# Stores on the GpSimd queue, bias tables loaded whole from reversed rows, two-head matmuls and a reordered first norm in a fused two-layer kernel

## The chip, the cores and the metric

One core of a Trainium2 chip runs the whole program. The metric is device time in microseconds (us) of one execution, the median over several.

## The reference

Two layers act on `x` of 1024 tokens by 1024 channels, in fp32, one after the other.

Layer 1: `h = rmsnorm(x) * norm_gain`, `proj = h @ w_in`, and two mixers. Eight heads of 64 attend over all tokens with two key heads (norm and axial rotation on q and k). Eight heads attend over a neighbourhood of 8 rows by 16 columns of a 64-wide grid, with a relative bias. Both are gated by `silu`, joined, multiplied by `w_out` and added to `x`; a final rmsnorm follows.

Layer 2: `rms_norm`, `h @ w_in_2`, and again two mixers: a gated delta rule (four heads of 128, chunks of 64, a triangular solve per chunk, a state carried along the tokens) and dilated attention:

```python
DILATED_PATTERNS = ((128, 1), (512, 4), (2048, 16))      # window, dilation
step = qi - kj + blk                                     # per residue class, current and previous block
scores = q . k + rel_bias[:, t5_bucket(step * r)]        # masked to 0 <= step <= window / r
lse = logsumexp(scores); p = exp(scores - lse); o = p @ v
o = sum over patterns of softmax(lse over patterns) * o  # then * silu(gate)
```

Both are joined, multiplied by `w_out_2` and added.

## The kernel before

**Numbers.** Projections split both operands into a high and a low part (`whi`, `wlo` for weights, `hh`, `hl` for activations) and sum three matmuls. Token tiles are 128 rows; activations are transposed on TensorE so that channels lie on partitions, and the evacuation writes `hh` on ScalarE and `hl = t - hh` on VectorE.

**Stages**, by the time of the profile: 0 to 49 us load of `x`, norm and 64 transposes (the loop at L547 to L575); up to 550 us the projections of layer 1 (`fill1`) woven with the first attention; up to 760 us neighbourhood attention woven with the output product; up to 850 us the rest of that product and the second norm; up to 1380 us the delta rule (`delta_main`), woven with the projections of layer 2 (`fill2`); then dilated attention (`jobs_c`, head pairs j = 0 to 3) woven with the last output product, to the end.

**What sets the order.** The program is written as two streams, `main` and `fill`, which `share` weaves by the TensorE time each has spent; a scheduler then fixes one static order for each engine. An engine, and each DMA queue, takes its instructions strictly in that order: a DMA issue that waits holds all issues behind it. Three names choose the queue: `ld` (loads) and `st` (stores) both issue from SyncE (SP), `gl` from GpSimd (POOL); `gl` carries only the loads of q, k and v for neighbourhood attention (L795, L796, L824). Stores and the loads that read them back go through tensors in device memory (`qa_d`, `bq_d`, `raw_d`, `ab_d`, `tb_d`, `n_d`, `yp_d`, `o_d`; names ending in `_d`).

**First norm.** `norm_gain` is loaded broadcast to 128 partitions (`ng`, L559). For tiles 2 to 7 VectorE multiplies each by it (L563); for tiles 0 and 1 the multiplication is fused with that by the row's scale (L574); the other scalings are three on VectorE (L572) and three on ScalarE (L570).

**Dilated attention.** `tables_c(j)` makes the bias tables of a pair of heads. `r_d` holds one row of 1024 numbers per head; table k needs, on partition p, the row shifted by p and reversed. A load brings the shifted piece into `trc` with step 1 (L1487), and a ScalarE copy writes it reversed into `tab` (L1489): six of each per pair, 24 in all. `item` (L1556) is one block of 128 queries of two heads: scores `s` (a high and a low pass per head), then on VectorE `Pc = -(s + tab)` with its row minimum (L1568), exponential on ScalarE (L1570), transposes, `PTc` copied on ScalarE (L1581), and `po = PTc^T vc` (P·V, 64 columns per head), copied to `N` or `Nst` (L1592). With dilation 8 (`nkt == 1`: 8 items) and the first blocks an item has one key block of 128, otherwise two. Results of two patterns go through `n_d` and are merged per half of the tokens in `union_c` (L1631 on).

**Memory.** The pool `wk` is closed after the delta rule (named "pd") and opened as "pc" over the same bytes; a new tile waits until the old tiles under it are free.

Of the kernel before, what the change touches and what calls it, by code (L numbers as in the profile page):

```python
# [32 lines left out]
NT = 8  # L33
KC = 8
# [28 lines left out]
XPR = 5000  # L63
XS = 1
LASTC = {1: 6, 2: 7}
# [11 lines left out]
CP = 'S'  # L77
CO = 'V'
CHP = 0
# [18 lines left out]
def shape_constants():  # L98
# [45 lines left out]
    for x in range(256):  # L144
# [3 lines left out]
        else:  # L148
            oh[32, 768 + x] = NEG
    return {"c1": c1, "c2": c2, "oh": oh}  # L150


@with_exitstack
def hybrid_kernel(ctx: ExitStack, tc: tile.TileContext, A, out, dbg=None, upto=99):
# [30 lines left out]
    ld = nc.sync.dma_start  # L185
    gl = nc.gpsimd.dma_start
    st = nc.sync.dma_start
    dbg = dbg or {}
# [352 lines left out]

    r_d = dp.tile([8, 1024], F32, name="r_d")


    w1 = A["w_in"][0]
    H = {}
    hr.open("h1")  # L547
    H1 = Tr(hr, KC)
    with tc.tile_pool(name="xp", bufs=2, reuse_waits="tile") as xp:
        ng = xp.tile([128, 1024], F32, name="ng", bufs=1)  # L550
        for b in range(0, NT, 2):
            ss = sm.tile([128, 2], F32, name="ssx")
            xg = []
            for i in (b, b + 1):
                xt = xp.tile([128, 1024], F32, name="xt", bufs=8)
                with tc.high_priority(XPR):
                    ld(xt, grid(x_in, i))
                    if i == 0:
                        ld(ng, dram(A["norm_gain"], 0, [[0, 128], [1, 1024]]))  # L559
                scr = xp.tile([128, 1024], F32, name="sqrow", bufs=1)  # L560
                S.activation(scr, xt, AF.Square, accum_out=ss[:, i - b:i - b + 1])
                if b:
                    V.tensor_tensor(xt, xt, ng, op=OP.mult)  # L563
                xg.append(xt)
            rs = rs_of(ss, 2, 1.0 / 1024)
            for i in (b, b + 1):
                xn = xg[i - b]
                r1 = rs[:, i - b:i - b + 1]
                if b and i % 2 and XS:
                    S.activation(xn, xn, AF.Copy, scale=r1)  # L570
                elif b:
                    V.tensor_scalar(xn, xn, r1, None, op0=OP.mult)  # L572
                else:
                    V.scalar_tensor_tensor(xn, xn, r1, ng, op0=OP.mult, op1=OP.mult)  # L574
                H1.put(xn, i)  # L575

    def make_bias():
        rb = wk.tile([33, 8], F32, name="rb")
        V.memset(rb, 1.0)
        tb8 = wk.tile([8, 32], F32, name="tb8")  # L580
        ld(tb8, A["rel_bias_2"])
        tb = tbank()
        PE.transpose(tb[0:32, 0:8], tb8, ident[0:8, 0:8])
        V.tensor_copy(rb[0:32], tb[0:32, 0:8])
        oh = wk.tile([33, 1024], F32, name="oh")
        ld(oh, A["oh"])
        rr = wk.tile([8, 1024], F32, name="rr")
# [4 lines left out]
        ld(r_d, rr)  # L592


    wk.open("rpp")
    if 1:
# [192 lines left out]
    def prep_b(j, B):  # L789
# [4 lines left out]
        for a in range(2):  # L794
            gl(k2[64 * a:64 * a + 64], dram(bq_d[j], (2 + a) * 128 * 1024, [[1024, 64], [64 * 1024, 2], [1, 1024]]))  # L795
        gl(vv, bv_d[j].rearrange("(t p) c -> p t c", p=128))  # L796
        if j == 0:
# [18 lines left out]
    def attn_b(j, B, live, then=None):  # L816
# [243 lines left out]
    def fill1():  # L1060
        ws, _ = load_w(w1, [(512, 0, 1, 256), (0, 0, 1, 256)])
# [91 lines left out]
    def delta_main():  # L1153
# [20 lines left out]
        def main2():  # L1174
# [164 lines left out]
            def chain(u):  # L1339
# [5 lines left out]
                for k in range(2):  # L1345
# [3 lines left out]
                    V.tensor_reduce(ac, am.rearrange("p t (b c) -> p t c b", c=16), op=OP.add, axis=AX.X)  # L1349
                    ld(dram(ab_d[u], k * 8192, [[16, 128], [2048, 4], [1, 16]]), ac)  # L1350
                Ab = wk.tile([64, 16, 16], F32, name="Ab")
# [6 lines left out]
                for r in range(1, 16):  # L1358
# [4 lines left out]
                    yield Y1  # L1363
                ld(tb_d[u], Tn.rearrange("p r c -> p (r c)"))

# [103 lines left out]
    yp_d = dp.tile([1024, 1024], F32, name="yp_d")  # L1469
    X, alt = {}, [0]  # L1470

# [72 lines left out]
    def jobs_c(j):  # L1544
# [5 lines left out]
        def values(n, *ap):  # L1550

            v = wk.tile([128, 8, 2, 64], F32, name="vc", bufs=VCB)
            ld(v.rearrange("p t h d -> p (t h d)").rearrange("p (a b) -> p a b", a=n), dram(cv_d[j], 0, list(ap)))
            return [v[:, t] for t in range(8)]

        def item(q, k, vs, T, N, then=None):  # L1556
# [9 lines left out]
            P = wk.tile([128, 2, 256], F32, name="Pc", bufs=CB)  # L1566
            for h in range(2):
# [9 lines left out]
            PT = wk.tile([128, 4, 128], F32, name="PTc", bufs=CB)  # L1577
            t3 = by4(tb[:, 0:2 * nkt * 128])
# [10 lines left out]
            if CO[alt[0] % len(CO)] == "S":  # L1589
                S.activation(N[:, 0:128], o[:, 0:128], AF.Copy)  # L1590
            else:
                V.tensor_copy(N[:, 0:128], o[:, 0:128])  # L1592
            if then:
# [3 lines left out]
        def nst():  # L1597
            return wk.tile([128, 2, 132], F32, name="Nst", bufs=NSB)

# [31 lines left out]
    def union_c(j):  # L1631
        def union(N0, b):

            Ns = [N0[:, 4 * b:4 * b + 4]]
            for p in range(2):
                N = wk.tile([128, 4, 132], F32, name="N%d" % (p + 1))
                ld(N, n_d[j][p][512 * b:512 * b + 512].rearrange("(t p) c -> p t c", p=128))
# [33 lines left out]
    def main():  # L1671
# [51 lines left out]
```

## Time and profile before

| | |
|---|---|
| median of 3 runs (lowest, highest) | 1762.08 us (1745.34, 1762.79) |
| profiled execution, its span | 1749.34 us, 1747.6 us |
| mean granted TensorE clock | 0.937 of full (2.4 GHz) |
| busy: TensorE, VectorE, ScalarE, GpSimd | 1560.6 (89%), 1121.8 (64%), 785.3 (45%), 28.5 us (2%) |
| DMA | 204.79 MB, 38.4% of 16 engines by hardware queue, 4.9% by the software queue of GpSimd |

A row of the timeline gives start, duration, engine, line, operation, tiles and shape; in brackets the idle time before it and what ended it. `SPq` is an issue on SyncE's queue. `--windows` rows give for a stretch the busy time of each engine with instruction counts, the granted TensorE clock (1.00 is 2.4 GHz, 0.50 is 1.2 GHz) and the busy share of the 16 DMA engines. PE is TensorE, DVE is VectorE, ACT is ScalarE.

### The profile page before, as it was taken

How to read it: one execution, taken by the hardware profiler on the slowest of the kernel's cores; microseconds unless marked ns; L12 is line 12 of the kernel's file. 1: busy time of each engine (PE TensorE's matmuls, PEld its weight loads, DVE VectorE, ACT ScalarE, POOL GpSimd, SP SyncE). 2: the span in 40 equal slices, each digit the busy share in tenths (PEclk: the TensorE clock that was granted, in tenths of full speed). 3: DMA queues.
4: the chain of work that ended last, by engine and by line, in shares of the span. 5: the costliest groups of instructions: out<-in, count | busy, mean ns of one | idle time of the engine just before them, and what ended most of it. 6: DMA issues, size and time to landing. Idle time of an engine off the chain costs nothing. (4 is left out here: it accounts for less than half of the span.)

```text
span 1747.6 us, 27569 instructions
## 1 busy us (share of the span) xinstructions
PE 1560.6 (89%) x9362; PEld 1377.5 (79%) x9362; DVE 1121.8 (64%) x3469; ACT 785.3 (45%) x2189; POOL 28.5 (2%) x48
## 2 busy tenths in 40 slices
PE   1988999999999789996799999998999489899997
PEld 1877788989898677885677788887889478788985
DVE  5679866666573554558545768676677575767646
ACT  5235445445452432544344443534524352765631
POOL 0000000000001101100000000000000000000000
PEclk8999999999999889997899999999999879876999
DMA  7011121422226998875344323314322555433476
GB/s 173 17 61 51 56 80 63 102 79 56 83 71 162 199 256 194 223 208 145 76 113 98 96 74 85 97 51 108 91 61 71 166 174 162 136 93 87 119 229 219
DMA packets 212825, 204.79 MB, mean 117 GB/s; under 512 B 27363, under 2 KB 164763, under 8 KB 212684
## 3 DMA queue, kind: packets, MB, share of 16 engines
q1 hardware_dynamic: 202252, 188.34, 38.4%
q0 software_dynamic: 10432, 14.68, 4.9%
q8 instruction: 74, 1.21, 0.3%
q14 instruction: 67, 0.55, 0.1%
HBM read 131.83 MB, written 71.13 MB: 116 GB/s over the span
## 5 line engine op out<-in xcount | busy, mean ns | idle before, releaser
L172 PE MATMUL pw<-whi,hh 128*128 128x512 f32 (+2 forms) x1032 | 359.1, 350 | 10.5 <-DVE e L524 5.4
L172 PE MATMUL pw<-wlo,hh 128*128 128x512 f32 (+2 forms) x1032 | 357.1, 346 | 0.3 <-DVE wlo L355 0.3
L172 PE MATMUL pw<-whi,hl 128*128 128x512 f32 (+2 forms) x1032 | 356.3, 345 | 0.0
L172 PEld LDWEIGHTS pw<-whi,hh 128*128 128x128 f32 x1032 | 196.9, 192 | 31.9 <-DVE e L524 6.0
L172 PEld LDWEIGHTS pw<-wlo,hh 128*128 128x128 f32 x1032 | 197.8, 192 | 19.6 <-DVE wlo L355 0.5
L172 PEld LDWEIGHTS pw<-whi,hl 128*128 128x128 f32 x1032 | 197.4, 191 | 19.9
L355 DVE TENSOR_TENSOR wlo<-e,whi 128x512 fp32r<-128x512 f32 (+3 forms) x168 | 103.6, 624 | 73.3 <-ACT whi L354 72.3
L354 ACT ACTIVATE whi<-e 128x512 fp32r<-128x512 f32 (+3 forms) x168 | 95.3, 581 | 96.9 <-DMA e<-in_w_in_dram 71.0
L172 PE MATMUL pw<-hh,whi 128*128 128x512 f32 x320 | 129.8, 405 | 7.6 <-ACT whi L354 7.5
L172 PE MATMUL pw<-hl,whi 128*128 128x512 f32 x320 | 127.2, 398 | 0.0
L172 PE MATMUL pw<-hh,wlo 128*128 128x512 f32 x320 | 123.3, 399 | 0.0
L172 PEld LDWEIGHTS po<-vc,PTc 128*128 128x128 f32 x560 | 87.9, 228 | 12.1 <-DVE N L1592 5.4
L172 PE MATMUL po<-vc,PTc 128*128 128x64 f32 x560 | 90.2, 304 | 7.3 <-DVE N L1592 4.2
L172 PE MATMUL s<-k,qT 128*128 128x512 f32 (+1 forms) x282 | 90.1, 407 | 2.7 <-ACT PT L845 1.3
L1568 DVE CUSTOM_DVE_ANT_0 Pc<-s,tab 128x128 f32<-128x128 f32 (+1 forms) x192 | 59.6, 348 | 39.5 <-PE s L172 26.4
L172 PE MATMUL po<-PT,vv 128*128 128x256 f32 x512 | 75.9, 288 | 3.9 <-DVE PT L745 3.2
L172 PEld LDWEIGHTS pw<-hh,whi 128*128 128x128 f32 x320 | 61.1, 191 | 23.2 <-ACT whi L354 11.2
L172 PEld LDWEIGHTS po<-PT,vv 128*128 128x128 f32 x512 | 68.7, 193 | 8.7 <-DVE PT L745 5.1
L745 DVE TENSOR_TENSOR PT<-s,PT 128x512 fp32r<-128x512 f32 x77 | 52.3, 685 | 32.2 <-ACT PT L744 23.1
L736 ACT ACTIVATE P<-s,nm 128x512 f32<-128x512 f32 x77 | 52.6, 686 | 44.7 <-DVE nm L733 41.9
L840 ACT ACTIVATE Pb<-Pb,m 128x384 f32<-128x384 f32 x64 | 39.1, 612 | 73.3 <-DVE m L838 70.6
L172 PEld LDWEIGHTS pw<-hl,whi 128*128 128x128 f32 x320 | 61.2, 191 | 11.4
(398 smaller groups left out, 3364.8 us busy)
## 6 DMA issues: line engine op xcount, KB each, us to landing
e<-in_w_in_dram SPq DMA_DIRECT2D x72, 256.0 KB, 3.7
bq_d<-e SPq DMA_DIRECT2D x32, 256.0 KB, 2.2
qT<-bq_d POOLq DMA_DIRECT2D x32, 256.0 KB, 7.4
e<-in_w_out_dram SPq DMA_DIRECT2D x32, 256.0 KB, 5.9
xp_d<-mx SPq DMA_DIRECT2D x32, 256.0 KB, 3.9
yp_d<-e SPq DMA_DIRECT2D x32, 256.0 KB, 3.3
e<-in_w_in_dram SPq DMA_DIRECT2D x32, 192.0 KB, 3.4
raw_d<-e SPq DMA_DIRECT2D x24, 256.0 KB, 2.0
```

The lines of the kernel that those rows point to most:

```text
L172: self.last = f(*a, **k).ins
L354: S.activation(hi[:, :n], raw[:, :n], AF.Copy)
L355: V.tensor_tensor(lo[:, :n], raw[:, :n], f32(hi[:, :n]), op=OP.subtract)
L736: S.activation(P[:, hf * 512:(hf + 1) * 512], ss[hf], AF.Exp, bias=nm[:, 2:3], accum_out=den[:, h, hf:hf + 1])
L745: V.tensor_tensor(dl, by4(tb), f32(dh), op=OP.subtract)
L840: S.activation(P, P, AF.Exp, bias=nm, scale=-1.0, accum_out=den[:, h:h + 1])
L1568: V.tensor_tensor_reduce(out=P[:, h, :nk], in0=sh[h], in1=T[:, h, T.shape[2] - nk:], op0=OP.add, op1=OP.min, scale=-1.0, scalar=3e38, accu ...
```

## The change

1. All stores (`st`) issue from GpSimd's software queue; all loads issue from SyncE, those of `gl` too.
2. The gain of the first norm is loaded as 8 rows of 128, transposed once to `gT`, and applied as a per-partition scale while the transposes are evacuated. Tiles are flipped in groups of 2, 2 and 4, and the first weights are loaded between them.
3. The one-hot rows behind the bias are kept reversed, `r_d` is copied to `rb_d` 128 times (4 MB, one DMA from GpSimd's queue) early in `fill1`, and each table is loaded whole with step 1023: no `trc`, no reversing copy.
4. Items with one key block compute scores against both heads' keys (256 columns instead of 128) and use the half that belongs; P·V multiplies with both heads' values (128 columns instead of 64); the copy to `N` picks the two right quarters.
5. When "pc" is opened, its tiles are allocated at once, in an order that lays them over the delta rule's tiles as those come free, the tables of pair 0 first.

```diff
-    gl = nc.gpsimd.dma_start
-    st = nc.sync.dma_start
+    st = nc.gpsimd.dma_start
...
+    oh = np.concatenate([oh[:, a:b][:, ::-1] for a, b in ((0, 384), (384, 768), (768, 1024))], 1)
...
-                if b:
-                    V.tensor_tensor(xt, xt, ng, op=OP.mult)
...
+        g8 = xp.tile([8, 128], F32, name="g8", bufs=1)
+        ld(g8, dram(A["norm_gain"], 0, [[128, 8], [1, 128]]))
...
+                    t, g = tb[:, k * n * 128:(k + 1) * n * 128], gT[:, k0 + k:k0 + k + 1]
+                    S.activation(h[:, k0 + k, c], t, AF.Copy, scale=g)
+                    V.scalar_tensor_tensor(l[:, k0 + k, c], t, g, f32(h[:, k0 + k, c]), op0=OP.mult, op1=OP.subtract)
...
+        for b in (0, 2):
+            normed(b)
+            flip_x((b, b + 1), gT)
+            if b == 0:
+                ws0 += load_w(w1, [(512, 0, 1, 256), (0, 0, 1, 256)])[0]
+                load_x(range(4, 8))
+        for b in (4, 6):
+            normed(b)
+        flip_x((4, 5, 6, 7), gT)
...
-            gl(k2[64 * a:64 * a + 64], dram(bq_d[j], (2 + a) * 128 * 1024, ...))
-        gl(vv, bv_d[j].rearrange("(t p) c -> p t c", p=128))
+            ld(f32(k2[64 * a:64 * a + 64]), dram(bq_d[j].bitcast(F32), (2 + a) * 128 * 1024, ...))
+        ld(vv, bv_d[j].rearrange("(t p) c -> p t c", p=128))
...
         yield from proj_q(0, ws, 256, rt, 2)
+        st(rb_d, dram(r_d, 0, [[1024, 8], [0, 128], [1, 1024]]))
...
-                tr = wk.tile([128, 256], F32, name="trc", bufs=2)
-                ld(tr[:, :w], dram(r_d, o + 384 * k, [[1, 128], [1, w]]))
-                rev = tr[:, w - 1::-1] if w == 256 else tr[:, 127::-1]
-                S.activation(T[:, h], rev, AF.Copy)
+                ld(T[:, h], dram(rb_d, (2 * j + h) * 131072 + 384 * k + 128, [[1023, 128], [1, T.shape[2]]]))
...
-            sh = [s[:, h * nk:(h + 1) * nk] for h in range(2)]
+            sh = [s[:, h * 256:(h + 1) * 256] for h in range(2)]
             for h in range(2):
-                PE.matmul(sh[h], qq[:, h, q], k2[:, h, k], start=True, stop=False)
-                PE.matmul(sh[h], ql[:, h, q], k2[:, h, k], start=False, stop=True)
+                kk = k2[:, h, k] if nkt == 2 else k2[:, :, k]
+                PE.matmul(sh[h], qq[:, h, q], kk, start=True, stop=False)
+                PE.matmul(sh[h], ql[:, h, q], kk, start=False, stop=True)
+            if nkt == 1:
+                sh = [s[:, h * 384:h * 384 + 128] for h in range(2)]
...
-                    PE.matmul(o[:, h * 64:h * 64 + 64], PT[:, h * nkt + t], v[:, h], start=t == 0, stop=t == nkt - 1)
+                    PE.matmul(o[:, h * 128:h * 128 + 128], PT[:, h * nkt + t], v.rearrange("p h d -> p (h d)"),
+                              start=t == 0, stop=t == nkt - 1)
...
         wk.open("pc")
+        X[0] = X[0][:3] + (tables_c(0),)
+        for n in ("Nst", "N1", "vc", "Pc", "N2"):
+            early[n] = tile_c(n)
+        wk.tile([128, 128], F32, name="gap")
+        early["PTc"] = tile_c("PTc")
```

The order moves at two places that matter below.

TensorE, where dilated attention begins: `e_...` are tiles of the delta rule's output being transposed for the last output product, `s<-da` scores, `s<-ident,Pc` transposes of an item, `po<-vc,PTc` its P·V. Before:

```order
L172 MATMUL pw<-ident,e_15381 128x128 x4
L172 MATMUL s<-da_13172,da_13173 128x128
L172 MATMUL s<-da_13172,da_13174 128x128
...
L172 MATMUL pw<-ident,e_15431 128x128 x4
L172 MATMUL s<-ident,Pc 128x128 x6
L172 MATMUL pw<-ident,e_15454 128x128 x4
L172 MATMUL s<-ident,Pc 128x128 x2
L172 MATMUL pw<-ident,e_15477 128x128 x4
```

After:

```order
L172 MATMUL pw<-ident,e_15350 128x128 x4
L172 MATMUL pw<-ident,e_15373 128x128 x4
L172 MATMUL s<-ident,Pc 128x128 x8
L172 MATMUL s<-da_13187,da_13188 128x256
L172 MATMUL s<-da_13187,da_13189 128x256
...
L172 MATMUL po<-vc,PTc 128x128 x2
...
L172 MATMUL s<-ident,Pc 128x128 x2
L172 MATMUL po<-vc,PTc 128x128 x4
L172 MATMUL s<-ident,Pc 128x128 x8
...
L172 MATMUL pw<-ident,e_15423 128x128 x4
```

Before, the transposes of `e_15431` (second half of the delta rule's tokens) stand ahead of the first item's transposes; now the transposes of several items and their P·V stand ahead of `e_15423`, the first of the second half.

SyncE at the same place, after the change (the tables of pair 0, then values and gate, then the tables of pair 1):

```order
L916 DMA e_15373<-o_d 128x512
L919 DMA e_15375<-g_d 128x512
L1524 DMA tab_13872<-rb_d 128x256
L1524 DMA tab_13873<-rb_d 128x256
L1524 DMA tab_13874<-rb_d 128x128
...
L1588 DMA vc<-cv_d_466 128x2x512
L1588 DMA vc<-cv_d_466 128x1024
L1693 DMA gtc<-g_d 128x4x128
...
L1556 DMA lqk<-c_d_463 128x2x256 x4
L916 DMA e_15423<-o_d 128x512
```

Before, the store `o_d<-orr` of the delta rule's last outputs stood in this queue ahead of the table loads; it now stands in GpSimd's queue.

## Rows read from the trace of the kernel before

**Rows 1.** The page, part 1: busy time, share of the span, instructions.

```profile
PE 1560.6 (89%) x9362; PEld 1377.5 (79%) x9362; DVE 1121.8 (64%) x3469; ACT 785.3 (45%) x2189; POOL 28.5 (2%) x48
```

**Rows 2.** Timeline, TensorE, 25 to 50 us.

```profile
26.30 1.08 PE L172 MATMUL s<-ident,xt 128*128 128x128 f32 x4 [26.30 <-DVE xt L574]
...
39.23 1.12 PE L172 MATMUL s<-ident,xt 128*128 128x128 f32 x4 [9.29 <-DVE xt L572]
...
49.28 0.39 PE L172 MATMUL pw<-whi,hh 128*128 128x256 f32 x1 [0.53 <-DVE rb L579]
```

**Rows 3.** Groups of instructions by form, 0 to 50 us: busy us, mean ns.

```profile
L563 DVE TENSOR_TENSOR xt<-xt,ng 128x1024 f32<-128x1024 f32 x6 | 7.3, 1224 | 3.1 <-ACT sqrow L561 3.0
...
L316 DVE TENSOR_TENSOR hl<-s,hh 128x512 fp32r<-128x512 f32 x8 | 5.4, 682 | 1.3 <-ACT hh L315 1.3
...
L574 DVE SCALAR_TENSOR_TENSOR xt<-xt,rq_y,ng 128x1024 f32<-128x1024 f32 x2 | 2.5, 1280 | 0.0
```

**Rows 4.** Waits of SyncE's queue: us in total, times, longest.

```profile
SPq L1098 <- ACT e L523: 114.3, 27, 11.1
```

**Rows 5.** Waits of TensorE: us in total, times, longest.

```profile
PE pw L172 <- ACT whi L354: 9.8, 7, 3.1
```

**Rows 6.** Timeline at the beginning of dilated attention, all engines.

```profile
1385.42 0.69 DVE L1451 TENSOR_TENSOR orr<-orr,dnw 128x512 f32<-128x512 f32 x1
1386.56 0.98 SPq L1487 DMA_DIRECT2D trc<-r_d  x2
...
1391.43 0.42 ACT L1489 ACTIVATE tab<-trc 128x256 f32<-128x256 f32 x1 [10.16 <-DMA trc<-r_d]
...
1392.94 0.29 DVE L1568 CUSTOM_DVE_ANT_0 Pc<-s,tab 128x128 f32<-128x128 f32 x1 [6.83 <-ACT tab L1489]
...
1403.86 1.08 PE L172 MATMUL pw<-ident,e 128*128 128x128 f32 x4 [23.89 <-DVE rq_ac L290]
```

**Rows 7.** Windows of dilated attention: busy us by engine, clock, DMA share, GB/s.

```profile
1495.00:1505.00 10.00, 9.30 (x41) 8.11 (x41) 6.16 (x24) 6.14 (x17) 0.00 (x0) 0.51 0.69 222
1538.00:1557.00 19.00, 18.35 (x90) 18.02 (x91) 10.02 (x49) 9.66 (x41) 0.00 (x0) 0.53 0.37 105
1592.00:1621.00 29.00, 26.56 (x126) 26.23 (x126) 14.42 (x67) 13.93 (x54) 0.00 (x0) 0.53 0.26 74
1621.00:1630.00 9.00, 8.95 (x78) 8.54 (x78) 4.60 (x23) 6.85 (x23) 0.00 (x0) 1.00 0.39 119
```

**Rows 8.** Timeline, 1606 to 1625 us: four score matmuls of an item.

```profile
1612.19 1.19 PE L172 MATMUL s<-da,da 128*128 128x128 f32 x4
...
1618.52 1.20 PE L172 MATMUL s<-da,da 128*128 128x256 f32 x4
```

**Rows 9.** P·V as a group, and timelines of eight matmuls at full clock.

```profile
L172 PE MATMUL po<-vc,PTc 128*128 128x64 f32 x560 | 90.2, 304 | 7.3 <-DVE N L1592 4.2
...
1704.18 1.00 PE L172 MATMUL po<-vc,PTc 128*128 128x64 f32 x8
...
1358.48 1.06 PE L172 MATMUL s<-Tt,d_kbe 128*128 128x128 f32 x8
```

**Rows 10.** Loads issued by GpSimd (ns on POOL; us to landing), and the page's stores issued by SyncE (KB, us to landing).

```profile
L824 POOL DMA_DIRECT2D qT<-bq_d x32: 610/626/655, 547.9 to 752.2; - x32
...
DMA to landing us min/median/max: 3.7/7.4/11.9
...
raw_d<-e SPq DMA_DIRECT2D x24, 256.0 KB, 2.0
```

**Rows 11.** A window between the bias rows' store and the first read-back.

```profile
75.00:100.00 25.00, 22.71 (x185) 21.83 (x185) 13.41 (x63) 6.94 (x21) 0.00 (x0) 1.00 0.00 1
```

**Rows 12.** Waits of VectorE for a read-back in the delta rule.

```profile
DVE tmpc L1393 <- DMA ac<-tb_d: 8.3, 4, 3.3
```

**Rows 13.** The chain that ended last, in order of time, near the end.

```profile
1690.87 6.33 DMA yp_d<-e
...
1700.14 4.70 DMA n_d<-Nst
```

More of the change, by code (lines that the diff above doesn't have):

```diff
@@ L77 @@
 CP = 'S'
-CO = 'V'
 CHP = 0
@@ L149, in shape_constants @@
             oh[32, 768 + x] = NEG
-    return {"c1": c1, "c2": c2, "oh": oh}
+    oh = np.concatenate([oh[:, a:b][:, ::-1] for a, b in ((0, 384), (384, 768), (768, 1024))], 1)
+    return {"c1": c1, "c2": c2, "oh": np.ascontiguousarray(oh)}
 @with_exitstack
@@ L542, in hybrid_kernel @@
     r_d = dp.tile([8, 1024], F32, name="r_d")
+    rb_d = dp.tile([8, 128, 1024], F32, name="rb_d")
     w1 = A["w_in"][0]
@@ L548, in hybrid_kernel, with load_x @@
     H1 = Tr(hr, KC)
+    ws0 = []
     with tc.tile_pool(name="xp", bufs=2, reuse_waits="tile") as xp:
[L550 to L554, printed above, removed]
+        g8 = xp.tile([8, 128], F32, name="g8", bufs=1)
+        ld(g8, dram(A["norm_gain"], 0, [[128, 8], [1, 128]]))
+        xts = []
+        def load_x(tiles):
+            for i in tiles:
                 xt = xp.tile([128, 1024], F32, name="xt", bufs=8)
@@ L557, in hybrid_kernel @@
                     ld(xt, grid(x_in, i))
[L558 to L561, printed above, removed]
-                if b:
-                    V.tensor_tensor(xt, xt, ng, op=OP.mult)
-                xg.append(xt)
-            rs = rs_of(ss, 2, 1.0 / 1024)
[L566 to L575, printed above, removed]
+                xts.append(xt)
@@ new lines, in normed @@
+        def normed(b):
+            ss = sm.tile([128, 2], F32, name="ssx")
+            for i in (b, b + 1):
+                scr = xp.tile([128, 1024], F32, name="sqrow", bufs=2)
+                S.activation(scr, xts[i], AF.Square, accum_out=ss[:, i - b:i - b + 1])
+            rs = rs_of(ss, 2, 1.0 / 1024)
+            V.tensor_scalar(xts[b], xts[b], rs[:, 0:1], None, op0=OP.mult)
+            if b < 4:
+                V.tensor_scalar(xts[b + 1], xts[b + 1], rs[:, 1:2], None, op0=OP.mult)
+            else:
+                S.activation(xts[b + 1], xts[b + 1], AF.Copy, scale=rs[:, 1:2])
@@ new lines, in flip_x @@
+        def flip_x(tiles, gT):
+            n = len(tiles)
+            h, l = H1.half(tiles[0] // 4)
+            c = slice(tiles[0] % 4 * 128, (tiles[0] % 4 + n) * 128)
+            m = 4 // n
+            for k0 in range(0, KC, m):
+                tb = wbank()
+                for k in range(m):
+                    for j, i in enumerate(tiles):
+                        PE.transpose(tb[:, (k * n + j) * 128:(k * n + j + 1) * 128], xts[i][:, (k0 + k) * 128:(k0 + k + 1) * 128], ident)
+                for k in range(m):
+                    t, g = tb[:, k * n * 128:(k + 1) * n * 128], gT[:, k0 + k:k0 + k + 1]
+                    S.activation(h[:, k0 + k, c], t, AF.Copy, scale=g)
+                    V.scalar_tensor_tensor(l[:, k0 + k, c], t, g, f32(h[:, k0 + k, c]), op0=OP.mult, op1=OP.subtract)
@@ new lines, in hybrid_kernel @@
+        load_x(range(4))
+        tb = tbank()
+        PE.transpose(tb[:, 0:8], g8, ident[0:8, 0:8])
+        gT = xp.tile([128, 8], F32, name="gT", bufs=1)
+        V.tensor_copy(gT, tb[:, 0:8])
+        for b in (0, 2):
[7 more added lines that the diff above has]
+        flip_x((4, 5, 6, 7), gT)
@@ L591, in make_bias @@
             V.tensor_copy(rr[:, c * 512:(c + 1) * 512], tb[0:8, :])
-        ld(r_d, rr)
+        st(r_d, rr)
     wk.open("rpp")
@@ L1060, in fill1 @@
     def fill1():
-        ws, _ = load_w(w1, [(512, 0, 1, 256), (0, 0, 1, 256)])
+        ws = ws0
         yield from proj_kv(ws, rt, kv)
@@ L1349, in chain @@
                     V.tensor_reduce(ac, am.rearrange("p t (b c) -> p t c b", c=16), op=OP.add, axis=AX.X)
-                    ld(dram(ab_d[u], k * 8192, [[16, 128], [2048, 4], [1, 16]]), ac)
+                    st(dram(ab_d[u], k * 8192, [[16, 128], [2048, 4], [1, 16]]), ac)
                 Ab = wk.tile([64, 16, 16], F32, name="Ab")
@@ L1363, in chain @@
                     yield Y1
-                ld(tb_d[u], Tn.rearrange("p r c -> p (r c)"))
+                st(tb_d[u], Tn.rearrange("p r c -> p (r c)"))
                 def join(mask, Tn_, Tt, H):
@@ L1469, in hybrid_kernel, with tile_c @@
     yp_d = dp.tile([1024, 1024], F32, name="yp_d")
-    X, alt = {}, [0]
+    X, alt, early = {}, [0], {}
+    shapes_c = {"Nst": ([128, 2, 132], NSB), "vc": ([128, 8, 2, 64], VCB), "Pc": ([128, 2, 256], CB), "PTc": ([128, 4, 128], CB),
+                "N1": ([128, 4, 132], 1), "N2": ([128, 4, 132], 1)}
+    def tile_c(n):
+        if n in early:
+            return early.pop(n)
+        shape, bufs = shapes_c[n]
+        return wk.tile(shape, F32, name=n, bufs=bufs)
     def load_gains():
@@ L1550, in values @@
         def values(n, *ap):
-            v = wk.tile([128, 8, 2, 64], F32, name="vc", bufs=VCB)
+            v = tile_c("vc")
             ld(v.rearrange("p t h d -> p (t h d)").rearrange("p (a b) -> p a b", a=n), dram(cv_d[j], 0, list(ap)))
@@ L1576, in item @@
                     PE.transpose(tb[:, (h * nkt + t) * 128:(h * nkt + t + 1) * 128], P[:, h, t * 128:(t + 1) * 128], ident)
-            PT = wk.tile([128, 4, 128], F32, name="PTc", bufs=CB)
+            PT = tile_c("PTc")
             t3 = by4(tb[:, 0:2 * nkt * 128])
@@ L1587, in item @@
                 for t, v in enumerate(vs):
-                    PE.matmul(o[:, h * 64:h * 64 + 64], PT[:, h * nkt + t], v[:, h], start=t == 0, stop=t == nkt - 1)
[L1589 to L1592, printed above, removed]
+                    PE.matmul(o[:, h * 128:h * 128 + 128], PT[:, h * nkt + t], v.rearrange("p h d -> p (h d)"),
+                              start=t == 0, stop=t == nkt - 1)
+            V.tensor_copy(N[:, 0:128].rearrange("p (h d) -> p h d", h=2), o.rearrange("p (a d) -> p a d", d=64)[:, 0::3])
             if then:
@@ L1597, in nst @@
         def nst():
-            return wk.tile([128, 2, 132], F32, name="Nst", bufs=NSB)
+            return tile_c("Nst")
         vs = values(2, [512, 128], [512 * 128, 2], [1, 512])
@@ L1635, in union @@
             for p in range(2):
-                N = wk.tile([128, 4, 132], F32, name="N%d" % (p + 1))
+                N = tile_c("N%d" % (p + 1))
                 ld(N, n_d[j][p][512 * b:512 * b + 512].rearrange("(t p) c -> p t c", p=128))
```

11 lines of the change are left out of this document (4 added, 7 removed).

## The prediction

> **What bounds the kernel now.** I read the page first, then the waits of TensorE and of SyncE's queue, then the stages one by one in the timeline and in windows. TensorE is busy 89% of the span [rows 1], so an edit pays only where TensorE stands still, or where it works at the lower clock. Three places show that. At the start TensorE waits for VectorE: it begins at 26.30 us, pauses 9.29 us before 39.23, and the first projection starts at 49.28 [rows 2]. Where dilated attention begins it stands still for 23.89 us before 1403.86 [rows 6]; the row names a rsqrt step of VectorE, but the rows before it tell the story: the store of the delta rule's outputs holds SyncE's queue, the load of the first table is issued at 1386.56, ScalarE waits 10.16 us for it, and VectorE forms its first `Pc` only at 1392.94. And within dilated attention three stretches of 10, 19 and 29 us run at a clock of 0.51 to 0.53, so at 1.2 GHz, though TensorE is busy for 9.30, 18.35 and 26.56 us of them [rows 7].
>
> The sum is made against the profiled execution, 1749.3 us; the median of the runs, 1762.1, lies 0.7% above it.
>
> **The first norm.** It removes from VectorE six multiplications by the gain, 7.3 us, and makes the two fused ones of 1280 ns [rows 3] into plain scalings, which the same loop's others show to be cheaper: at most 2.5 us. It adds one small copy, one more scaling of a tile on VectorE instead of ScalarE, and eight more evacuations, since 16 of the 512-column ones of 682 ns become 16 of 256 and 8 of 512 columns. If a half-width one costs between half and the whole of 682 ns, these eight add between 0 and 5.5 us. Net VectorE loses between 2 and 9 us ahead of the first projection; its start depends on VectorE [rows 2], but also on the landing of `x`, which stays, less half a megabyte of `ng`. I take **-4 us** (-1 to -8), nearer to the low end because the last tiles arrive when they arrive.
>
> **Stores to GpSimd's queue, loads all on SyncE.** What goes: loads no longer stand behind a store that waits for its data. SyncE waited 114.3 us for the evacuations of one projection alone [rows 4], but TensorE waited only 9.8 us for weights [rows 5]; the e5 buffers loaded ahead hide the rest. So at most 9.8 us, of which I take **-3 us**, since loads now wait in SyncE's queue for read-backs (q, k and v of neighbourhood attention among them, formerly off it). What comes: each store is written by software. GpSimd takes 610 to 655 ns per load of the trace [rows 10] and has little else to do, 28.5 us in the whole span [rows 1]; some 400 stores at 0.63 us are 250 us, spread. Landing is the price: 2.0 us for a store of SyncE, against 3.7 at the least and 7.4 at the median for GpSimd's loads [rows 10]. Those loads are cut into rows of 256 elements, most stores into longer ones, so a store is nearer the low end: I take +1.7 us per store. It is exposed where a read-back is waited for. In the delta rule that is seen: 8.3 us in four waits for `ac<-tb_d` [rows 12]. Four such trips and four of `ab_d` at +1.7 are 14 us, of which TensorE is covered by the woven projections for most; **+3 us** (0 to +14 here).
>
> Whether VectorE holds GpSimd up is the other risk. All 32 issues of GpSimd took between 610 and 655 ns [rows 10] while VectorE was at work beside them. The Trainium skill, SBUF — State Buffer, the box on the "DVE blocks DMA" trap, says that GpSimd cannot write descriptors while VectorE runs a two-port operation and puts an issue so held at about 3100 instead of 620 ns; no issue here shows it, and by that rule stores would land later still, which is the slower rival below.
>
> The copy `rb_d` is 4 MB and stands in GpSimd's queue ahead of the first `qa_d` store. Its window is empty: from 75 to 100 us the DMA engines moved 1 GB/s [rows 11]. At the 222 GB/s of the busiest window above [rows 7], 8 MB of reads and writes are 38 us; **0 us**. If it took 20 us more, the first attention's read-backs would stand for that long: kept for the slower rival.
>
> **Tables.** 24 loads and 24 copies become 24 loads. The copies of 0.42 us [rows 6] leave ScalarE, 9 us in all, off TensorE's path. What counts is the beginning: SyncE's queue no longer holds the store, the tables have their place before the delta rule ends, and the first `Pc` waits only for VectorE, which ends `orr` at 1386.11 [rows 6]. One `Pc` and an exponential later, about 1388, TensorE transposes the first item, where it began at 1403.86: up to 16 us. The order now puts several items ahead of the transposes of the second half, so they cover the later landing of `o_d`. But items there run at VectorE's and ScalarE's pace, so not all 16 us are filled with TensorE's work. **-11 us** (-5 to -16).
>
> **Two-head matmuls.** They add columns that are thrown away. Four score matmuls of 128 columns with step 8 take 1.19 us and four of 256 columns 1.20 [rows 8]: 0. For P·V, eight of 64 columns take 1.00 us and eight of 128 take 1.06 [rows 9]; 560 at 0.0075 us are **+4 us**. The Trainium skill, TensorE: Matmul & The Clock Gate, Back-to-back issue gap, gives some 60 cycles up to 64 columns and 134 for 128; by it the 560 would cost 17 us. The two rows differ by 7.5 ns, not 31, so by them something else than columns sets the pace.
>
> What they can return is the clock. In each of the three slow stretches TensorE works without a break on narrow matmuls; in the last, 1.00 is granted from 1621 on [rows 7], right after the scores became 256 wide at 1618.52 [rows 8]. I read that as cause, not chance, since the same kind of item with wide scores then runs at full clock. 58 us at half clock hold 54.2 us of TensorE work, 27 at full clock; VectorE has 30.6 us and ScalarE 29.7 there, so 58 can fall to some 31: -27 at best, 0 if the clock stays. I take **-20** for the clock, and with the +4 it is **-16 us** (+4 to -27).
>
> **The end.** The chain ends through a store and read-backs: 6.33 us for `yp_d<-e`, 4.70 for `n_d<-Nst` [rows 13]. Both move to the software queue, +1.7 to +5.4 each (7.4 less 2.0), and the last stores to `out` too, while loads of `N` no longer stand behind stores. **-2 us** (+11 to -9).
>
> **The sum**: -4 - 3 + 3 - 11 - 16 - 2 = -33, so **1716 us**, 2.6% below the median.
>
> **Rivals.**
> 1. *The clock doesn't rise.* For it: one change of clock after one change of width is thin evidence. Then the term is +4 instead of -16: **1736 us**. Chance 0.17.
> 2. *The gap moves.* The tiles of "pc" still wait for the last delta tiles, or the tables for SyncE's read-back of `o_d`, so that TensorE stands as before at 1380. Then the 11 us are not won: **1727 us**. Against it: in the new order the tables stand ahead of the second half's loads. Chance 0.14.
> 3. *P·V is paid by the column.* If each of the 64 added columns costs a clock at 2.4 GHz, 27 ns, the 560 cost 15 us instead of 4: **1727 us**. The pair of timelines [rows 9] speaks against it; the skill's section named above speaks for it. Chance 0.05.
> 4. *Slower: software stores are late.* By the code, 16 read-backs of `qa_d`, 8 of the delta rule and 16 of `n_d` are 40 trips; if a store lands 5.4 us later (7.4 less 2.0) [rows 10], that is 216 us of latency, and GpSimd's queue passes it on in order, as SyncE's did. With a third of it on TensorE's path the sum is 1716 + 72 = **1788 us**; it decides against the change from a quarter on (54 us). Against it: the order was made with lead, and the trace's covers are long. Chance 0.12.
>
> The forecast itself has 0.52.
>
> **How the numbers follow.** The terms' lower ends give 1749 - 8 - 9.8 - 16 - 27 - 9 = 1680, but not all at once: **1684**. Upwards rivals 1 and 2 together reach 1747, and the high bound of the delta rule's trips adds 10: **1757**. Rival 4 lies outside. What a measurement can tell from no change is about 1%, 17 us round the median: faster means below 1744.5. The forecast and most of rivals 1 to 3 lie there: **0.77**; what is left of them and a mild form of rival 4: **0.14**; slower **0.09**.
>
> **What would show it.** The first projection at about 45 us; TensorE at work again by 1390 less what was won before; a clock of 1.00 through the items with dilation 8; issues on GpSimd at about 0.63 us and stores landing within 4 us; no new wait of TensorE behind `qa`, `ac` or `N`. The forecast is wrong if TensorE waits for a read-back for more than 30 us in all, or if the clock stays at 0.5 with the wide scores.

## The result and the profile after

The changed kernel takes 1690.6 us (median of 4 runs, 1686.5 to 1696.4) where the kernel before, run beside it, takes 1755.7: a ratio of 0.964 [0.957, 0.970]. Its profiled execution has a span of 1684.7 us at a mean granted clock of 0.968, against 1747.6 at 0.937. The forecast was 1716, its range 1684 to 1757.

To see where 63 us went, the two traces are laid side by side by events that both have. The rows below are answers by tile: duration minimum, median and maximum in ns, then the start of the first and of the last. They are the exponentials of neighbourhood attention (`Pb`), the copies of the delta rule's output (`orr`) and the first VectorE step of dilated attention (`Pc`). The kernel before:

```profile
L840 ACT ACTIVATE Pb<-Pb,m x64: 598/615/620, 564.8 to 783.0; 128x384 f32<-128x384 f32 x64
L1445 DVE COPY orr<-po x32: 266/279/284, 1069.8 to 1378.1; 128x128 f32<-128x128 f32 x32
L1568 DVE CUSTOM_DVE_ANT_0 Pc<-s,tab x192: 241/292/426, 1392.9 to 1714.7; 128x128 f32<-128x128 f32 x104, 128x256 f32<-128x256 f32 x88
```

After:

```profile
L870 ACT ACTIVATE Pb<-Pb,m x64: 599/616/636, 554.7 to 755.8; 128x384 f32<-128x384 f32 x64
L1476 DVE COPY orr<-po x32: 266/280/284, 1044.7 to 1347.7; 128x128 f32<-128x128 f32 x32
L1607 DVE CUSTOM_DVE_ANT_0 Pc<-s,tab x192: 278/292/427, 1357.8 to 1646.5; 128x128 f32<-128x128 f32 x104, 128x256 f32<-128x256 f32 x88
```

Differences of neighbouring events give the stages:

| stretch, up to | before | after | won |
|---|---|---|---|
| first projection's start | 49.3 | 44.2 | 5.1 |
| first `Pb` | 564.8 | 554.7 | 5.0 more |
| last `Pb` (neighbourhood attention) | 783.0 | 755.8 | 17.1 more |
| last `orr` (delta rule) | 1378.1 | 1347.7 | 3.2 more |
| first `Pc` | 1392.9 | 1357.8 | 4.7 more |
| last `Pc` (dilated attention) | 1714.7 | 1646.5 | 33.1 more |
| end of span | 1747.6 | 1684.7 | 5.3 lost |

A stretch of one profile is no sharp measure. From the first to the last `Pb`, seven profiles whose code for that stage is the changed kernel's (this one and e2, e3, e6, e7, e9 and e12 below) take between 194.1 and 204.2 us. From the last `orr` to the end this profile takes 337.0 us, e9 339.4, and e10, with the same code there, 349.8. So 5 to 10 us in one stretch are no finding.

**The start**, which answers to [rows 2]: TensorE's timeline.

```profile
14.74 0.45 PE L172 MATMUL s<-ident,xt 128*128 128x128 f32 x1 [14.74 <-DVE xt L570]
...
31.61 1.09 PE L172 MATMUL s<-ident,xt 128*128 128x128 f32 x4 [7.26 <-DVE hl L590]
...
44.20 0.39 PE L172 MATMUL pw<-whi,hh 128*128 128x256 f32 x1 [1.32 <-DVE hl L590]
```

Transposes start 11.6 us earlier, the first projection 5.1.

**The beginning of dilated attention**, which answers to [rows 6]:

```profile
1347.62 2.83 SPq L1524 DMA_DIRECT2D tab<-rb_d  x6
...
1357.20 0.69 DVE L1482 TENSOR_TENSOR orr<-orr,dnw 128x512 f32<-128x512 f32 x1
...
1357.81 0.28 DVE L1607 CUSTOM_DVE_ANT_0 Pc<-s,tab 128x128 f32<-128x128 f32 x1
...
1358.76 1.50 POOL L1483 DMA_DIRECT2D o_d<-orr  x2 [26.20 <-DVE Nst L1607]
...
1359.18 2.12 PE L172 MATMUL s<-ident,Pc 128*128 128x128 f32 x8 [6.54 <-ACT Pc L1609]
```

The tables are issued 9.6 us before VectorE begins its last step on `orr`; the first `Pc` follows that step at once, and TensorE waits 6.5 us where it waited 23.9. The store of `o_d` is issued only at 1358.76, but no load stands behind it in its queue.

**Dilated attention**, which answers to [rows 7]: two windows (busy us of TensorE, its weight loads, VectorE, ScalarE and GpSimd with counts; clock; DMA share; GB/s).

```profile
1475.00:1500.00 25.00, 24.23 (x156) 23.00 (x157) 15.33 (x84) 16.42 (x66) 5.30 (x8) 1.00 0.36 107
1540.00:1560.00 20.00, 19.95 (x146) 19.39 (x146) 10.76 (x61) 15.28 (x60) 3.63 (x6) 1.00 0.35 110
```

The clock is 1.00 through both. TensorE does 146 matmuls in the 20 us from 1540; in the window from 1538 the kernel before did 90 in 19 us at 0.53, though the two windows do not hold quite the same items.

**The software queue**, which answers to [rows 10]: GpSimd's issues of one store by tile, and DMA issues of the whole run (KB, median us to landing).

```profile
L524 POOL DMA_DIRECT2D g_d<-e x88: 537/538/572, 188.4 to 1332.0; - x88
...
qT<-bq_d SPq DMA_DIRECT2D x32, 256.0 KB, 7.8
...
raw_d<-e POOLq DMA_DIRECT2D x24, 256.0 KB, 2.4
xp_d<-mx POOLq DMA_DIRECT2D x32, 256.0 KB, 4.7
n_d<-Nst POOLq DMA_DIRECT2D x32, 132.0 KB, 2.8
```

Most stores cost GpSimd 0.54 us. From SyncE, `raw_d` landed in 2.0 us, `xp_d` in 3.9 and `n_d` in 3.2, so the software queue is 0.8 us later in one case and 0.4 us earlier in another. The loads of q land in 7.8 us from SyncE's hardware queue: the 7.4 us of [rows 10] were those of that transfer, not those of software.

### The profile page after: what moved, and what is told of

Same layout as the page of the kernel before. It is cut to its first block, busy times and chain, and to the rows that moved or that the text cites. A ratio compares the mean times of both kernels' runs of the same rounds, so it can differ in the third digit from the quotient of the medians.

```text
span 1684.7 us, 27850 instructions
## 1 busy us (share of the span) xinstructions
PE 1533.9 (91%) x9363; PEld 1351.4 (80%) x9363; DVE 1118.6 (66%) x3473; ACT 775.3 (46%) x2172; POOL 262.3 (16%) x475
## 4 chain that ended last, share of the span: by engine, by line
issue 42%; PE 33%; POOL 8%; DVE 7%; DMA 7%; ACT 3%; SPq 0%; POOLq 0%; DVEq 0%; ACTq 0%
PE pw L172 19%; PE s L172 9%; PE po L172 3%; PE p L172 2%; POOL g_d L524 1%; POOL o_d L646 1%; DMA xt<-in_x_dram 1%; POOL bv_d L799 1%; POOL xp_d L950 1%; DMA e<-in_w_in_dram 1%; POOL o_d L895 1%; DVE wlo L354 1%; DMA e<-g_d 1%; DMA lqk<-c_d 1%; DVE hl L590 1%
## 5 line engine op out<-in xcount | busy, mean ns | idle before, releaser
L172 PE MATMUL po<-vc,PTc 128*128 128x128 f32 x560 | 83.3, 285 | 7.3 <-DVE N L1630 7.0
L172 PEld LDWEIGHTS po<-vc,PTc 128*128 128x128 f32 x560 | 76.0, 200 | 11.4 <-DVE N L1630 6.3
L172 PEld LDWEIGHTS pw<-hh,whi 128*128 128x128 f32 x320 | 60.5, 189 | 26.9 <-ACT whi L353 15.1
L766 ACT ACTIVATE P<-s,nm 128x512 f32<-128x512 f32 x77 | 52.5, 685 | 51.0 <-DVE nm L763 49.3
L1609 ACT ACTIVATE Pc<-Pc,Nst 128x128 f32<-128x128 f32 (+1 forms) x128 | 53.7, 421 | 37.7 <-DVE Nst L1607 36.3
L172 PEld LDWEIGHTS pw<-hh,wlo 128*128 128x128 f32 x320 | 60.1, 189 | 11.6
```

The lines of the kernel that those rows point to most:

```text
L172: self.last = f(*a, **k).ins
L766: S.activation(P[:, hf * 512:(hf + 1) * 512], ss[hf], AF.Exp, bias=nm[:, 2:3], accum_out=den[:, h, hf:hf + 1])
L1609: S.activation(P[:, h, :nk], P[:, h, :nk], AF.Exp, bias=N[:, 128 + h:129 + h], scale=-1.0, accum_out=N[:, 130 + h:131 + h])
```

## The experiments

All ratios are to the kernel before, run beside each on the same chip; the changed kernel has 0.964 [0.957, 0.970].

**e1: the stores back on SyncE.**

```diff
-    st = nc.gpsimd.dma_start
+    st = nc.sync.dma_start
```

> The changed kernel with all stores back on SyncE's queue (all loads there too, the 4 MB copy of the bias rows as well). Against 1691 us for the changed kernel. Theory A (the 17 us that neighbourhood attention won, and some 5 each before and after it, come from loads that no longer stand behind stores): 1710 to 1720 us, with the last exponential of neighbourhood attention back at about 775 us instead of 756. Rival (those 17 us come from q, k and v being loaded by hardware instead of by GpSimd's software, the stores' queue is worth nothing): 1688 to 1695 us.

Measured: 1721.3 us, ratio 0.985 [0.980, 0.991]. So the stores' queue is worth 2.1% of the time before, some 37 us (1 to 3.4% by the ends of the two intervals). That is Theory A, by time just above its range, though the last exponential comes earlier than the 775 it named. The trace has its last `Pb` at 769.5 (against 755.8), its last `orr` at 1362.4 (1347.7), its last `Pc` at 1672.3 (1646.5), its end at 1712.5 (1684.7): 14 us are lost up to the end of neighbourhood attention, 11 in dilated attention with its beginning, little elsewhere. TensorE's waits near the beginning of dilated attention (us in total, times, longest):

```profile
PE s L172 <- DVE Nst L1607: 11.5, 1, 11.5
```

**e2: narrow matmuls.** Both edits of `item` undone: the scores use `k2[:, h, k]` with 128 columns, P·V `v[:, h]` with 64.

```diff
-                kk = k2[:, h, k] if nkt == 2 else k2[:, :, k]
...
+                PE.matmul(sh[h], qq[:, h, q], k2[:, h, k], start=True, stop=False)
...
-                    PE.matmul(o[:, h * 128:h * 128 + 128], PT[:, h * nkt + t], v.rearrange("p h d -> p (h d)"),
...
+                    PE.matmul(o[:, h * 64:h * 64 + 64], PT[:, h * nkt + t], v[:, h], start=t == 0, stop=t == nkt - 1)
```

> The changed kernel with narrow score and P.V matmuls as before (128 and 64 columns), all else kept. Theory B (wide matmuls keep the clock up in dilated attention): stretches at a clock of about 0.5 come back, some 40 to 60 us of them, and the time is 1707 to 1720 us. Rival (the clock rose because the stage is fed better, the width is nothing): clock near 0.98 throughout the stage as in the changed kernel, 1686 to 1692 us.

Measured: 1703.9 us, ratio 0.975 [0.970, 0.980]. The half clock is back, in the same windows as above:

```profile
1475.00:1500.00 25.00, 23.33 (x117) 23.01 (x116) 12.93 (x67) 12.25 (x46) 4.13 (x6) 0.57 0.28 88
1540.00:1560.00 20.00, 19.36 (x90) 18.77 (x90) 10.38 (x49) 9.52 (x36) 3.23 (x5) 0.50 0.25 79
```

Theory B holds for the clock; the time lies just below its range and clear of the rival's. By the ratios width is worth about 1.1%, 20 us, with intervals that touch. In the profiles the stretch from the last `orr` to the end is 350.0 us against 337.0 (and 339.4 in e9), but e10, whose matmuls are wide, takes 349.8 there, so the profiles do not show this gain by themselves.

**e3: no early allocation.**

```diff
-        X[0] = X[0][:3] + (tables_c(0),)
-        for n in ("Nst", "N1", "vc", "Pc", "N2"):
-            early[n] = tile_c(n)
-        wk.tile([128, 128], F32, name="gap")
-        early["PTc"] = tile_c("PTc")
```

> The changed kernel without the early allocation in pool pc (tables and work tiles are allocated where they are first used), all else kept. Theory C (the order of the tiles lets dilated attention begin at once): TensorE's wait at its beginning grows from 6.5 us to 15 to 20, time 1700 to 1705 us. Rival (the gap went with the stores on GpSimd's queue and the missing reversal): 1689 to 1694 us.

Measured: 1687.5 us, ratio 0.967 [0.962, 0.973], which overlaps the changed kernel's. Its longest wait of TensorE there is again 6.5 us. Theory C falls: the order of the buffers is worth nothing that these runs can measure.

**e4: the kernel before with wide matmuls alone**, the edit of e2 the other way round.

> The kernel before with the wide matmuls alone. Against 1756 us of before. Theory B: the three stretches at half clock go, 1732 to 1742 us. Rival (width is nothing): 1754 to 1760 us with the half-clock stretches still there; if the added columns cost what they cost at full clock by the column, 1771 us.

Measured: 1739.1 us, ratio 0.996 [0.993, 0.998]. The stretches of [rows 7] run at full clock:

```profile
1538.00:1557.00 19.00, 17.21 (x138) 16.24 (x137) 12.46 (x67) 16.18 (x61) 0.00 (x0) 1.00 0.38 109
1592.00:1621.00 29.00, 26.84 (x194) 25.22 (x193) 19.48 (x105) 20.81 (x76) 0.00 (x0) 1.00 0.32 94
```

Half of the expectation: the clock does what Theory B says, but the time falls by 8 us, not by 14 to 24 (1739.1 lies in the named range only because the kernel before took 1746.8 beside it). From the last `orr` to the last `Pc` it wins 11.6 us (336.6 to 325.0); from there to the end it takes 41.9 instead of 32.9 and gives 9 back. The wait of 24 us at the beginning stays (23.7).

**e5: the kernel before with its stores on GpSimd's queue alone** (the one line of e1, the other way round).

> The kernel before with its stores on GpSimd's queue as the one edit (q, k and v of neighbourhood attention stay on that queue too, four small stores stay on SyncE). Ratio to before; the whole change has 0.964. Theory A (a stores' queue of its own is the largest single part): 0.978 to 0.986, neighbourhood attention some 10 us shorter and the wait at the beginning of dilated attention down from 24 us to about 12. Rival (it only pays together with q, k and v on SyncE, because those loads now stand behind stores): 0.995 or more.

Measured: 1732.1 us, ratio 0.984 [0.978, 0.990]: Theory A, 28 us without any other part. Neighbourhood attention (first to last `Pb`) takes 211.5 us where it took 218.2 (and 217.0 in e4, with the same code there): less than the 10 named, and no more than profiles of one kernel differ. More is won in dilated attention: from the last `orr` to the last `Pc` 313.6 us against 336.6, of which the end gives 14 back (47.3 against 32.9). The wait is not down to 12:

```profile
PE pw L172 <- DVE rq_ac L290: 19.6, 1, 19.6
```

**e6 and e7: wide scores alone, wide P·V alone**, each one of the two edits of e2.

> The changed kernel with wide scores and narrow P.V (64 columns). Ratio to before; the changed kernel has 0.964, both narrow 0.975. Theory B1 (the score matmuls with step 8 are what lowers the clock): no stretch of half clock, 0.963 to 0.966. Rival B2 (the 64-column P.V matmuls lower it): half clock as with both narrow, 0.973 to 0.977.

> The changed kernel with wide P.V and narrow scores. Theory B1: half clock as with both narrow, ratio 0.973 to 0.977. Rival B2: no half clock, 0.963 to 0.966. If both are needed, both this and the mirror run show half clock in part, 0.967 to 0.972.

Measured: wide scores alone 1687.8 us, ratio 0.961 [0.956, 0.965]; wide P·V alone 1703.8, ratio 0.970 [0.965, 0.974]. By time, the scores carry it. By clock neither does alone: each still has stretches below full (0.88 from 1475 to 1500 with wide P·V), with wide scores

```profile
1480.00:1500.00 20.00, 19.80 (x129) 19.13 (x130) 9.63 (x60) 13.70 (x55) 3.65 (x6) 0.87 0.33 95
1535.00:1550.00 15.00, 14.16 (x68) 13.61 (x68) 6.60 (x35) 7.17 (x31) 2.76 (x4) 0.61 0.38 116
```

so the expectation of no half clock fails, and still the time is that of the changed kernel. Nor does the clock tell these two runs apart: the mean granted clocks of their timed runs are 0.955 to 0.964 and 0.953 to 0.962, their medians 16 us apart. And from the first to the last `Pc` the profile of wide scores takes 288.6 us at a mean clock of 0.90, that of the changed kernel 288.7 at 0.98. So width changes both the clock and the time, but that it changes the time by way of the clock is not shown. Whether wide P·V adds anything to wide scores, these runs leave open.

**e8: q, k and v of neighbourhood attention on GpSimd again**, all else as changed.

```diff
+    gl = nc.gpsimd.dma_start
...
-                ld(f32(qTs[b][64 * a:64 * a + 64]), dram(bq_d[j].bitcast(F32), b * 256, ...))
+                gl(f32(qTs[b][64 * a:64 * a + 64]), dram(bq_d[j].bitcast(F32), b * 256, ...))
```

> The changed kernel with the loads of q, k and v of neighbourhood attention back on GpSimd's queue, now among the stores. With stores on SyncE that attention took 212 us, in the changed kernel 201, before 218: so these loads should be worth the other 6 us. Theory: neighbourhood attention 206 to 210 us, ratio 0.967 to 0.970. Rival (the loads stand behind stores that wait, on one queue): 0.975 or more. Other rival (nothing): 0.962 to 0.966.

Measured: 1713.4 us, ratio 0.974 [0.969, 0.979]: close to the rival. First to last `Pb` takes 213.9 us (201.1). GpSimd's queue shows why:

```profile
573.74 0.54 POOL L896 DMA_DIRECT2D o_d<-oa  x1 [0.79 <-DVE oa L894]
579.82 1.25 POOL L855 DMA_DIRECT2D qT<-bq_d  x2 [5.55 <-PE s L172]
581.07 0.56 POOL L896 DMA_DIRECT2D o_d<-oa  x1
```

A load of q waits 5.55 us until TensorE has freed its buffer, and the next store of `o_d`, which had no wait of its own left, is issued only behind it. Loads wait for buffers and stores for data; on one queue each can hold the other, on GpSimd's here as on SyncE's in [rows 6].

**e9: the changed kernel again**, beside the next three.

> The changed kernel once more, on the chip of the three runs beside it, so that they are compared with it and not only with the kernel before. Ratio to before 0.957 to 0.970.

Measured: 1696.3 us, ratio 0.966 [0.961, 0.970].

**e10: the first norm as before.**

> The changed kernel with the first norm as before (gain broadcast, multiplied on VectorE). Theory: the first projection starts at 49 instead of 44 us and the 5 us pass through to the end: 4 to 6 us above the changed kernel, ratio up by 0.003. Rival (the later work absorbs them, since its waits for DMA then shrink): no difference.

Measured: 1696.8 us, ratio 0.967 [0.963, 0.971], not to be told from e9. Its first projection starts at 46.9 us and not at 49, e9's at 44.4: of the 5.1 us won at the start, the new norm accounts for 2.5. Whether they reach the end is open.

**e11: the tables as before**, without the 4 MB copy.

```diff
-        st(rb_d, dram(r_d, 0, [[1024, 8], [0, 128], [1, 1024]]))
...
-                ld(T[:, h], dram(rb_d, (2 * j + h) * 131072 + 384 * k + 128, [[1023, 128], [1, T.shape[2]]]))
...
+                ld(tr[:, :w], dram(r_d, (2 * j + h) * 1024 + 384 * k, [[1, 128], [1, w]]))
+                rev = tr[:, w - 1::-1] if w == 256 else tr[:, 127::-1]
+                S.activation(T[:, h], rev, AF.Copy)
```

> The changed kernel with the bias tables as before: shifted pieces of one row loaded into a work tile and reversed on ScalarE, no 4 MB copy; tiles still allocated early, stores still on GpSimd. TensorE's wait at the beginning of dilated attention was 24 us before, 19.6 with only the stores moved, 11.5 in the changed kernel with stores on SyncE, 6.5 in the changed kernel. Theory: whole tables close most of the gap, so it is back at 15 to 20 us and the time is 8 to 13 us above the changed kernel. Rival (the queue of the stores closes it): within 3 us.

Measured: 1711.6 us, ratio 0.975 [0.971, 0.980], 15 us above e9. TensorE's wait at the beginning of dilated attention:

```profile
PE pw L170 <- DVE rq_ac L287: 15.3, 1, 15.3
```

Theory, and somewhat more: 8 to 9 us of the 15 are this wait. The others are not traced; I put them down to the tables being loaded through two work tiles in turn. The next rows, from 11 us later, show one such wait (ScalarE waits 4.31 us for a piece, then VectorE for ScalarE):

```profile
1372.37 0.61 ACT L1524 ACTIVATE tab<-trc 128x256 f32<-128x256 f32 x2 [4.31 <-DMA trc<-r_d]
...
1372.82 0.42 DVE L1607 CUSTOM_DVE_ANT_0 Pc<-s,tab 128x256 f32<-128x256 f32 x1 [0.89 <-ACT tab L1524]
```

**e12: a shorter end.**

```diff
-                st(out[i * 128:(i + 1) * 128, c * 512:c * 512 + 512], y)
+                ld(out[i * 128:(i + 1) * 128, c * 512:c * 512 + 512], y)
...
-            put(to, slice(0, 128), od3[i // 4][:, i % 4].rearrange("p h d -> p (h d)"), 0, 1, 0.5)
+            if i == 4:
+                seq["w"] = ["pw", "s", "p"]
+            for q in ([i] if i % 4 == 0 else []) + ([i + 1] if i % 4 < 3 else []):
...
+                put(tos[q], slice(0, 128), od3[q // 4][:, q % 4].rearrange("p h d -> p (h d)"), 0, 1, 0.5)
```

> The changed kernel with another end: the stores to the output on SyncE's queue, the transpose of the next 128 tokens ahead of the products of the present ones, and three kinds of PSUM banks instead of one for the last four tiles. At the end of the changed kernel each tile takes 2.5 us, of which TensorE 1.7 and VectorE 1.7; its last store lands 4.3 us after it is issued. Theory: 0.5 to 0.8 us per tile and 1 us at the end, 4 to 7 us below the changed kernel. Rival (the merges on VectorE set the end): within 2 us.

Measured: 1687.2 us, ratio 0.961 [0.957, 0.965], 9 us below e9 by the medians, with intervals that overlap. In the trace the stretch from the last `Pc` to the end is 33.6 us (38.5 in e9, 38.2 in the changed kernel): 5 us, as expected, though e10, with the changed kernel's end, takes 46.4 there at a mean clock of 0.69. A gain over the changed kernel is likely, not proved.

## Why the prediction was right, and where its sizes were off

The direction and the range held; the gain was twice the forecast (65 us by the medians, against 33 in the sum). That the range held is in part luck: its low end counted on up to 27 us from the clock, which could not come (point 5), and on at most 9.8 us from the stores, which brought several times that. Most signs named came true: first projection at 44.2 us, TensorE at work in dilated attention from 1359.2, issues of 0.54 us. One did not: `xp_d` lands in 4.7 us, above the 4 named. The parts as measured below overlap, so they do not add up to the whole.

1. **First norm, -4.** The trace shows -5.1 at the first projection, of which 2.5 belong to the norm (e10); e10 cannot tell whether they reach the end.
2. **Stores and loads, -3 and +3: the step that failed.** It is worth 37 us by e1 and 28 alone by e5. It was mis-sized twice. The gain was bounded by one row, TensorE's wait for weights [rows 5]. That wait did not even fall: it is 14.1 us now. What stands behind a store is every load of a stage, and TensorE's waits there carry other names. Neighbourhood attention, 17 us shorter, has no weight wait in its list. Waits of TensorE over the whole run, before:

```profile
PE s L172 <- ACT Pb L840: 13.6, 7, 4.2
PE po L172 <- DVE oa L863: 7.5, 2, 4.0
```

After:

```profile
PE pw L172 <- ACT whi L353: 14.1, 13, 3.1
PE s L172 <- ACT Pb L870: 7.8, 7, 3.7
```

The stage as a window, before and after:

```profile
564.80:783.00 218.20, 188.97 (x1111) 167.90 (x1110) 109.80 (x324) 90.20 (x237) 21.47 (x34) 0.90 0.90 216
554.70:755.80 201.10, 183.90 (x1109) 162.19 (x1108) 108.33 (x324) 88.84 (x236) 36.10 (x67) 0.93 0.82 235
```

TensorE stands still for 17 us in it instead of 29, and is busy 5 us less, at a somewhat higher mean clock. Which load freed which wait isn't traced. The price was taken from the only rows of the software queue, the loads of q [rows 10]. The same loads land in 7.8 us from SyncE, so the row told of the transfer; the stores land between 0.4 us earlier (`n_d`) and 0.8 later (`xp_d`), where the term had +1.7. Moving q, k and v off GpSimd was called a cost for SyncE; e8 shows that leaving them among the stores would cost 16 to 19 us (against e9 and the first runs), and the order of waits in the queue is the reason its rows show.
3. **The 4 MB copy, 0.** It landed 23.5 us after its issue at 55.7, ahead of the first `qa_d` store at 104.5: hidden, as the empty window said.
4. **Tables and their tiles, -11.** e11: 15 us, of which 8.8 are the wait at the beginning, inside the 5 to 16 named for it; the whole change takes that wait from 23.9 to 6.5. The term left out that something is won behind the beginning too. The mechanism was part right: reversal and queue close the gap; the tiles' order, on which the step also rested, does nothing (e3).
5. **Two-head matmuls, -16.** The clock rose, as forecast, for the reason given (e2, e4). By time, width is worth 8 us (e4) to 20 us (e2); that the clock is what brings them, as the term had it, is not shown (e6, e7). The best case of -27 could not come: it halved all work of TensorE in these stretches. Scores with step 4 or 8 are not paced by the clock. In e2, at 0.50, four narrow ones take 0.98 us from start to next start:

```profile
1545.18 1.18 PE L172 MATMUL s<-da,da 128*128 128x128 f32 x4
1546.16 0.64 PE L172 MATMUL s<-ident,Pc 128*128 128x128 f32 x2
```

In e7, at 1.00, four narrow ones take 1.01, as long:

```profile
1549.69 1.19 PE L172 MATMUL s<-da,da 128*128 128x128 f32 x4
1550.70 0.29 PE L172 MATMUL s<-ident,Pc 128*128 128x128 f32 x1
```

In the changed kernel, at 1.00, four wide ones take 1.11, and eight of P·V with 128 columns follow:

```profile
1540.37 1.29 PE L172 MATMUL s<-da,da 128*128 128x256 f32 x4
1541.48 1.07 PE L172 MATMUL po<-vc,PTc 128*128 128x128 f32 x8
```

What got faster at the higher clock is P·V and the transposes. Groups of the changed kernel, 1445 to 1640 us (busy us, mean ns):

```profile
L172 PE MATMUL po<-vc,PTc 128*128 128x128 f32 x400 | 58.5, 280 | 3.8 <-DVE N L1630 3.6
L172 PE MATMUL s<-ident,Pc 128*128 128x128 f32 x198 | 40.0, 278 | 0.8 <-DVE M L1678 0.6
```

The same of e2:

```profile
L172 PE MATMUL po<-vc,PTc 128*128 128x64 f32 x404 | 71.5, 327 | 2.4 <-DVE N L1626 2.2
L172 PE MATMUL s<-ident,Pc 128*128 128x128 f32 x198 | 46.9, 332 | 2.6 <-ACT Pc L1606 1.4 <-DVE Nst L1626 0.9 <-ACT hh L311 0.3
```

Twice the columns for 13 us less; all scores of the window together take about 98 us in both. Rival 3, P·V by the column, compares widths at one clock: eight of 128 columns take 1.07 us here against 1.00 for eight of 64 [rows 9], or 5 us for 560, so it is refuted. By the table of the Trainium skill, TensorE: Matmul & The Clock Gate, Back-to-back issue gap, an estimate is 17 us; the two rows speak against it for this stream.

6. **The end, -2.** It became +5.3, and in e4 the same stretch took back 9 us of 12. The term looked at stores and read-backs, but the loss lies elsewhere. After the last `Pc`, 48 matmuls of the output product are left in both kernels. Before, the first of them starts 6.0 us after the last `Pc`, among the last P·V (a row of the timeline, and one of TensorE's waits in this stretch):

```profile
1720.67 0.77 PE L172 MATMUL pw<-whi,mth 128*128 128x512 f32 x1
...
PE po L172 <- DVE N L1592: 0.5, 1, 0.5
```

After, it starts 11.2 us after it, behind all P·V, and TensorE waits longer for the copies of P·V's results in this stretch:

```profile
1657.73 0.49 PE L172 MATMUL pw<-whi,mth 128*128 128x512 f32 x1 [0.37 <-ACT mth L311]
...
PE po L172 <- DVE N L1630: 3.4, 4, 1.6
```

From that matmul to the end it is 26.9 us before and 27.0 after, so the whole loss is ahead of it. In e4, with wide matmuls alone, it starts 13.1 us after the last `Pc`. Why the order came out so is open.
7. **Rivals.** Rival 1, no rise of the clock: refuted; the clock is 1.00 in the windows above, and e2 shows that width raises it. Rival 2, the gap moves: 6.5 us are left, so refuted in the main. Rival 4, late software stores: refuted, its price of 5.4 us per store was 0.8 at most in the rows above. The Trainium skill, SBUF — State Buffer, the box on the "DVE blocks DMA" trap, stood for it; none of the 88 stores of `g_d` took GpSimd more than 572 ns, though VectorE is busy for 66% of the span. The box speaks of two-port operations of VectorE; whether any ran beside a store isn't read from the trace, so these stores do not test it. The figures of 620 and 3100 ns that the prediction took from that page for an issue stand there for a whole transfer, in the section behind the box.

## What to carry to other kernels

Try a queue of their own for the stores before tuning what waits for loads, and put no load that waits for a buffer among them. Take the price of a queue from the same transfer on both queues, not from the only transfer that happens to use it. A wait's name in the profile tells what came last, not what the queue held up: bound the gain by the whole stage, not by one row.

## What was not expected of the hardware

TensorE ran for 20 us at 1.2 GHz while busy for 19.4 of them, on narrow matmuls (e2), and at 2.4 GHz in the same window with wide ones. With wide scores and narrow P·V (e6) it still fell to 0.50 while busy from 1544 to 1550 us. Four score matmuls with a step cost about as much at either clock: 0.98 us (e2, at 0.50) and 1.01 (e7, at 1.00) with 128 columns, 1.10 (e6, at 0.50, from 1545.99) and 1.11 (the changed kernel, at 1.00) with 256.
